# Alternating the two experts' gate and up products, and a new place for the transposed dense input

## The chip, the cores and the metric

The kernel runs on one core of one Trainium2 chip. The metric is the device time of one execution in microseconds. Three timed runs of the kernel before gave 1130.45, 1132.79 and 1132.81 us, so a median of 1132.79 us. The profiled execution took 1131.38 us, and its span from the first to the last instruction is 1129.59 us.

## The reference

A batch of one sequence of 256 tokens of width 1024 passes through two blocks. The first has a gated delta rule and a differential attention side by side, and a dense SwiGLU feed-forward of width 2816. The second has gated linear attention and block attention side by side, then cross attention to a memory, then a mixture of 32 experts, and a last RMS norm. The experts are what the change is about:

```
expert = grp * EXPERTS_PER_GROUP + top_i            # 2 experts per token
hid = jax.nn.silu(xb @ w_gate[e]) * (xb @ w_up[e])  # 1024 -> 512, twice
out += (hid @ w_down[e]) * w[:, None]               # 512 -> 1024
```

Everything is float32. One expert has 3 x 1024 x 512 weights, so the 32 of them are 201 MB, and all of them are read from HBM.

## The kernel before, in words

All tokens sit in two tiles of 128. Up to about 640 us of the span the kernel does the dense work; every weight of it is streamed through three raw buffers (`wr0` to `wr2`, pool `raw`), split into a high and a low part (`wh`, `wl`, pool `hl`, four of each) and multiplied against the transposed input (`xTh`, `xTl`, pool `xt`, eight tiles of 2 KB per partition). These pools, with `cst2`, `m1` and `g1` below them, lie on the left side of SBUF, one above the other in the order in which they are opened.

The experts then run in 16 pairs. Per expert 64 tokens are gathered (`CAP`), so one expert fills half of the 128 output partitions: expert j of a pair writes partitions `H[j]`, 0 to 63 or 64 to 127. For one pair, the loop at line 2197 does:

- at every other pair a `gather` for the next two pairs (`ohr` against `xh` and `xl`), then `hid_T`, the transposes of the hidden rows;
- `gate_up` of the next pair (line 2097): for 8 slices k of 128 input rows, gate (c = 0) and up (c = 1) of both experts, 32 matmuls with 64 columns of `xe` as the weights of the array and 512 columns of expert weights moving. The profile records each of these float32 matmuls as two, so 64 records. After the first quarter of them `between` puts in the `combine` of the pair before (`ys` against `pwT`) and `slots_T`;
- `down` of this pair (line 2121): 16 matmuls (32 records), in the order k, c, j, so that it alternates between the experts.

The last pair has no next one. In its place come `final_gain`, `between` and two fillers (`keep`). After the loop come `combine`, the norm and the stores.

The expert weights arrive in units of 1 MB: four of gate and up (q = 0 to 3, two k each, two transfers of 512 KB) and two of down per expert. They are loaded by SP's queue in the order in which the pairs use them: gate and up of pair p + 1, then down of pair p; within them q by q, first expert 0, then expert 1. The last two units are cut in two halves each. There are 22 slots of 8 KB per partition (tiles `wm`). Four are opened early, five after the mixer, and 13 when the left pools are closed; these 13 (`rawl`, `wm0` to `wm12`) lie over what was `m1`, `g1`, `xt`, `hl` and `raw`. The list at line 804 is the order in which those 13 are filled, and each waits for whoever last used the bytes below it. A unit can only be loaded into a slot when the unit 22 places earlier in the order has been used up.

The order of matmuls on TensorE is that of the program text (no planner acts in the expert part). Every engine instruction is recorded at line 249, since one helper issues them all.

Of the kernel before, what the change touches and what calls it, by code (L numbers as in the profile page):

```python
# [138 lines left out]
RAW = 3  # L139
HLB = 4  # L140
NXT = 8
# [280 lines left out]
class K:  # L422
# [338 lines left out]
    def build(self):  # L761
        tc = self.tc
        with ExitStack() as top:
            P = lambda name, bufs, **kw: top.enter_context(tc.tile_pool(name=name, bufs=bufs, **kw))
            self.c = P("cst", 1)
            psum = P("psum", 1, space=PSUM)
            self.dram = P("dram", 1, space=DRAM)
            self.sm = P("sm", 2)
            work = P("work", 1)
            self.xe = work.tile([128, 8, 4, CAP], F32, name="xe")  # L770
            self.hdT = work.tile([128, 4, 2 * CAP], F32, name="hdT")
            self.sg = work.tile([128, 512], F32, name="sg")
            top.enter_context(tc.manual_schedule())
            self.banks = [psum.tile([128, 512], F32, name=f"bank{i}") for i in range(8)]
            self.freeb, self.turn = list(self.banks), 0
            prj = ExitStack()
            Q = lambda name, bufs: prj.enter_context(tc.tile_pool(name=name, bufs=bufs, side="left"))
            self.c2 = Q("cst2", 1)
            self.M1 = Q("m1", NM1)
            self.G1 = Q("g1", NG1)  # L780
            self.XT = Q("xt", NXT)
            self.hl = Q("hl", 1)
            self.raw = Q("raw", 1)
            with tc.tile_pool(name="g2a", bufs=NG2A, side="right") as self.G2:
                self.rt = None
                self.begin()
                self.block1_attn()
            self.experts = Experts(self, P("early", 1, side="right", reuse_waits="tile"))
            with tc.tile_pool(name="g2", bufs=NG2, side="right", reuse_waits="tile") as self.G2:
                self.S.after = lambda: self.experts.load(min(self.experts.n + NAFT, NRE))  # L790
                self.block1_ffn()
                out = self.mixer()
            self.rt = P("rt", 1, side="right", reuse_waits="tile")
            self.experts.more(P("rawt", 1, side="right", reuse_waits="tile"), reversed(range(NRT)))
            self.S.after = lambda: self.experts.load(self.experts.n + NAFT)
            self.S.after()
            self.drive(self.norm_, [out])
            self.mem_attn()
            prj.close()
            A = P("moe", 1, side="left", reuse_waits="tile")  # L800
            raw = lambda i: 10 + (len(self.S.units) - i) % RAW
            hl = lambda i: 6 + (len(self.S.pieces) - i) % HLB
            self.experts.more(P("rawl", 1, side="left", reuse_waits="tile"),
                              [0, raw(3), raw(2), 5, 4, raw(1), hl(4), hl(3), hl(2), hl(1), 1, 2, 3])
            self.experts.early = False
            self.moe(A)

# [1237 lines left out]
    def moe(self, A):  # L2045
# [51 lines left out]
        def gate_up(n, j0, ws_, between=None):  # L2097

            g = [self.bank() for _ in range(2)]
            for k, j, c in [(2 * q + i, j, c) for q in range(4) for j in range(n) for i in range(2) for c in range(2)]:  # L2100
                if between and (k, j, c) == (2, 0, 0):
                    between()
                self.mm(g[c][H[j]], xe[:, k, j0 + j], ws_(j, k // 2)[:, c, k % 2], k == 0, k == 7)
            sg = self.sg
            R = slice(0, n * CAP)
            nc.scalar.activation(sg[R], g[0][R], AF.Silu)
            V.tensor_tensor(sg[R], g[1][R], sg[R], op=ALU.mult)
            return sg
# [76 lines left out]
        quad = lambda p: rk[:, :, 2 * p:min(2 * p + 4, NE)]  # L2185
        gather(2, self.oh, [x])
        hd = gate_up(2, 0, unit(0))
        for t in range(2):
            nc.scalar.activation(xh[t], x[t], AF.Copy, scale=self.r[:, t:t + 1])
# [7 lines left out]
        for p in range(NP):  # L2197
            n = min(4, NE - 2 * (p + 1))
            if p % 2 == 0 and n:
                gather(n, oh, [xh, xl])  # L2200
            hdT = hid_T(2, hd)
            pw = one_hot(2, col(rk, p), col(W32, p))
            if p % 2 and p + 2 < NP:
                oh = hot(quad(p + 2), min(4, NE - 2 * (p + 2)))

            def between():
                nonlocal pT
                if p:
                    combine(pT)
                pT = slots_T(2, pw)  # L2210
            if n:
                hd = gate_up(2, 2 * (p % 2), unit(p + 1), between)
                X.load(12 * p + 16 + NR)
            else:
                final_gain()
                between()
                keep(NLAST)
            down(2, hdT, unit(p))
            X.load(12 * p + 20 + NR)
# [5 lines left out]
        with tc.If(most > CAP):  # L2225
            with tc.For_i(0, NE, 1) as e:
                one = bass.ds(e, 1)
                rke = A.tile([128, 2, 2], F32, name="rke")
                V.tensor_copy(rke[:, 0, :, None], rk[:, :, one])
                V.tensor_copy(rke[:, 1, :, None], W32[:, :, one])  # L2230
                wu = [X.fetch(spare[q], one, q) for q in range(6)]
                rk_, w_ = (lambda t, j: rke[:, 0, t:t + 1]), (lambda t, j: rke[:, 1, t:t + 1])
                for _ in range(1, T // CAP):
                    V.tensor_scalar(rke[:, 0], rke[:, 0], -float(CAP), None, op0=ALU.add)
                    gather(1, hot(rke[:, 0, :, None], 1), [xh, xl])
                    pT = slots_T(1, one_hot(1, rk_, w_))
                    down(1, hid_T(1, gate_up(1, 0, lambda j, q: wu[q])), lambda j, q: wu[q])
                    for c in range(2):
                        for t in range(2):
                            b = self.bank()  # L2240
                            for i in range(2):
                                self.mm(b, pT[H[0], t * 128:(t + 1) * 128], ys[c][i][H[0]], i == 0, i == 1)
                            sum_ = spare[7 + c][:, t * 512:(t + 1) * 512]
                            nc.scalar.activation(sum_, acc[t][c], AF.Copy)
                            V.tensor_tensor(acc[t][c], b, sum_, op=ALU.add)
            norm_first()
            norm_out()
# [27 lines left out]
```

## Time and profile before

| what | value |
|---|---|
| median of three runs | 1132.79 us |
| profiled execution | 1131.38 us |
| its span | 1129.59 us |
| PE busy | 1107.8 us (98%) |
| DVE, ACT busy | 504.1 us (45%), 381.2 us (34%) |
| read from HBM | 297.83 MB, 265 GB/s over the span |
| gate and up records (`wm`, `xe`) | 1024, first at 640.6 us, last at 1097.2 us |
| down records (`wm`, `hdT`) | 512, first at 682.3 us, last at 1116.4 us |

Busy PE time is a weak measure here: the end of a matmul is modelled, and a matmul on one half of the array counts as busy as two on both halves. What a stretch costs is better read from the starts of what stands before and after it.

### The profile page before, as it was taken

What the parts mean: (1) busy time and instruction counts of PE and PEld (TensorE: products, weight loads), DVE (VectorE), ACT (ScalarE), POOL (GpSimd) and SP (SyncE); (2) the same over time, 40 slices, a digit from 0 to 9 for tenths busy, and PEclk for the clock granted to TensorE, in tenths of its full rate; (3) what the DMA queues carried; (4) which work ended last, traced back from release to release, by engine and by line L of the source; (5) the groups of instructions that cost most, each with busy time, mean ns of one, the idle gap of its engine ahead of it and who ended that gap; (6) DMA issues with size and microseconds to landing.
All of it is one profiled execution on the core that took longest, in us unless ns stands there. A gap on an engine that the chain in (4) does not pass through costs nothing.

```text
span 1129.6 us, 16831 instructions
## 1 busy us (share of the span) xinstructions
PE 1107.8 (98%) x6850; PEld 784.5 (69%) x6850; DVE 504.1 (45%) x917; ACT 381.2 (34%) x678; POOL 57.3 (5%) x85
## 2 busy tenths in 40 slices
PE   9999999999999999999999989999999999999996
PEld 8989788999999887989988644444444445444453
DVE  5777756656556576665666321212121212111112
ACT  6553556544344475565454210000000000000103
POOL 0153011000000010100000000000000000000000
PEclk9999999999999999999999999999999999999999
DMA  8454216674664544545498689999999999999931
GB/s 299 136 165 133 76 38 199 254 246 167 197 189 162 172 150 152 179 126 180 161 359 335 243 337 407 411 413 411 413 412 413 413 413 414 413 413 413 415 156 40
DMA packets 105950, 300.06 MB, mean 266 GB/s; under 512 B 6999, under 2 KB 35980, under 8 KB 97932
## 3 DMA queue, kind: packets, MB, share of 16 engines
q1 hardware_dynamic: 104700, 295.23, 69.6%
q0 software_dynamic: 1024, 3.17, 1.0%
q8 instruction: 56, 0.92, 0.3%
q10 hardware_dynamic: 144, 0.52, 0.1%
q14 instruction: 26, 0.21, 0.1%
HBM read 297.83 MB, written 1.07 MB: 265 GB/s over the span
## 4 chain that ended last, share of the span: by engine, by line
PE 93%; DVE 3%; ACT 2%; issue 1%; DMA 0%; POOL 0%; SPq 0%; ACTq 0%; DVEq 0%
PE bank L249 93%; ACT junk L249 1%; DVE cy L249 0%; DMA x<-in_x 0%; DVE junk L249 0%; DVE xTl L249 0%; ACT wh L249 0%; DVE x L249 0%; DVE xl L249 0%; ACT xTh L249 0%; DVE wm L249 0%; ACT sg L249 0%; DVE dp L249 0%; POOL nr L249 0%; DVE smz L249 0%
## 5 line engine op out<-in xcount | busy, mean ns | idle before, releaser
L249 PE MATMUL bank<-wm,xe 128*64 128x512 f32 x1024 | 285.1, 598 | 0.0
L249 DVE TENSOR_TENSOR wl<-wr,wh 128x1024 fp32r<-128x1024 f32 (+1 forms) x175 | 211.0, 1222 | 134.2 <-ACT wh L249 130.8
L249 PE MATMUL bank<-xTh,wh 128*128 128x256 f32 x768 | 223.1, 291 | 0.0
L249 ACT ACTIVATE wh<-wr 128x1024 fp32r<-128x1024 f32 (+1 forms) x175 | 180.1, 1050 | 118.2 <-PE bank L249 104.6
L249 PE MATMUL bank<-xTl,wh 128*128 128x256 f32 x768 | 217.3, 283 | 0.8 <-DVE xTl L249 0.8
L249 PE MATMUL bank<-xTh,wl 128*128 128x256 f32 x768 | 217.1, 283 | 0.2 <-DVE wl L249 0.2
L249 PEld LDWEIGHTS bank<-wm,xe 128*64 128x64 f32 x1024 | 101.0, 136 | 160.3 <-issue 157.1
L249 PEld LDWEIGHTS bank<-xTh,wh 128*128 128x128 f32 x768 | 147.0, 191 | 4.6 <-issue 2.4
L249 PEld LDWEIGHTS bank<-xTl,wh 128*128 128x128 f32 x768 | 147.1, 192 | 2.3 <-DVE xTl L249 1.2
L249 PEld LDWEIGHTS bank<-xTh,wl 128*128 128x128 f32 x768 | 147.0, 191 | 0.4 <-DVE wl L249 0.4
L249 PE MATMUL bank<-wm,hdT 128*64 128x512 f32 x512 | 128.7, 595 | 0.0
L249 ACT ACTIVATE sg<-bank 128x512 f32<-128x512 f32 x20 | 11.9, 597 | 295.3 <-PE bank L249 295.2
L249 DVE TENSOR_TENSOR sg<-bank,sg 128x512 f32<-128x512 f32 x16 | 11.1, 691 | 191.7 <-PE bank L249 191.7
L249 PEld LDWEIGHTS bank<-wm,hdT 128*64 128x64 f32 x512 | 46.5, 137 | 65.9 <-issue 60.7
L249 DVE SCALAR_TENSOR_TENSOR ys<-bank,ws,ys 128x512 fp32r<-128x512 f32 x32 | 24.0, 751 | 98.8 <-ACT ys L249 96.9
L249 ACT ACTIVATE ys<-bank,ws 128x512 fp32r<-128x512 f32 x32 | 22.0, 688 | 106.1 <-PE bank L249 106.1
L249 DVE TENSOR_SCALAR pwT<-bank 128x256 fp32r<-128x256 f32 x16 | 6.8, 424 | 90.1 <-PE bank L249 90.1
L249 POOL TENSOR_TENSOR nr<-nr,mhalf 128x2 f32<-128x2 f32 (+1 forms) x9 | 6.0, 673 | 713.0 <-DVE nr L249 712.9
L249 PE MATMUL bank<-wl,fhh 128*128 128x512 f32 x88 | 35.2, 400 | 0.0
L249 PE MATMUL bank<-wh,fhh 128*128 128x512 f32 x88 | 34.8, 395 | 0.0
L249 PEld LDWEIGHTS bank<-ys,pwT 128*128 128x128 f32 x128 | 22.8, 188 | 17.2 <-issue 11.4
L249 PE MATMUL bank<-ys,pwT 128*128 128x512 f32 x128 | 34.3, 408 | 0.3 <-DVE ys L249 0.3
(386 smaller groups left out, 1477.0 us busy)
## 6 DMA issues: line engine op xcount, KB each, us to landing
wm<-in_w_exp_gate SPq DMA_DIRECT2D x128, 512.0 KB, 10.2
wm<-in_w_exp_up SPq DMA_DIRECT2D x128, 512.0 KB, 10.2
wm<-in_w_exp_down SPq DMA_DIRECT2D x62, 1024.0 KB, 12.6
wr<-in_w_in SPq DMA_DIRECT2D x33, 1024.0 KB, 5.2
wr<-in_w_gate_up SPq DMA_DIRECT2D x22, 1024.0 KB, 5.7
wr<-in_w_down SPq DMA_DIRECT2D x11, 1024.0 KB, 5.1
wr<-in_w_out SPq DMA_DIRECT2D x8, 1024.0 KB, 5.1
wr<-in_w_ckv SPq DMA_DIRECT2D x4, 1024.0 KB, 6.3
```

What stands on the lines that cost most here:

```text
L249: r = f(*args, **kw)
```

## The change

Two edits. In `gate_up` the 32 matmuls of a pair come in another order: before, for each unit quarter q, all four matmuls of expert 0 and then all four of expert 1; after, for each k and c, one of expert 0 and one of expert 1. The sums that are formed are the same, and `between` stands at the same place (k = 2). The pool `xt` is opened after `hl` and `raw` and not ahead of them, so that it lies above them; the list of the left slots is renumbered so that its entries name the same buffers in the same order.

```
@@ -778,9 +778,9 @@
             self.M1 = Q("m1", NM1)
             self.G1 = Q("g1", NG1)
-            self.XT = Q("xt", NXT)
             self.hl = Q("hl", 1)
             self.raw = Q("raw", 1)
+            self.XT = Q("xt", NXT)
@@ -798,10 +798,10 @@
-            raw = lambda i: 10 + (len(self.S.units) - i) % RAW
-            hl = lambda i: 6 + (len(self.S.pieces) - i) % HLB
+            raw = lambda i: 8 + (len(self.S.units) - i) % RAW
+            hl = lambda i: 4 + (len(self.S.pieces) - i) % HLB
             self.experts.more(P("rawl", 1, side="left", reuse_waits="tile"),
-                              [0, raw(3), raw(2), 5, 4, raw(1), hl(4), hl(3), hl(2), hl(1), 1, 2, 3])
+                              [0, raw(3), raw(2), 12, 11, raw(1), hl(4), hl(3), hl(2), hl(1), 1, 2, 3])
@@ -2097,8 +2097,8 @@
-            for k, j, c in [(2 * q + i, j, c) for q in range(4) for j in range(n) for i in range(2) for c in range(2)]:
-                if between and (k, j, c) == (2, 0, 0):
+            for k, c, j in [(k, c, j) for k in range(8) for c in range(2) for j in range(n)]:
+                if between and (k, c, j) == (2, 0, 0):
                     between()
                 self.mm(g[c][H[j]], xe[:, k, j0 + j], ws_(j, k // 2)[:, c, k % 2], k == 0, k == 7)
```

On TensorE, at the start of `gate_up` of pair 1 (the first of its kind with a `between`), the program's order differs as follows; `wm_5657` is the unit of expert 2, `wm_6218` that of expert 3, `bank_77` takes the gate and `bank_81` the up product.

```order
 L249 MATMUL bank_76<-cst_109,sg 128x128 x4
 L249 MATMUL bank_77<-wm_5657,xe 64x512
+L249 MATMUL bank_77<-wm_6218,xe 64x512
 L249 MATMUL bank_81<-wm_5657,xe 64x512
+L249 MATMUL bank_81<-wm_6218,xe 64x512
 L249 MATMUL bank_77<-wm_5657,xe 64x512
+L249 MATMUL bank_77<-wm_6218,xe 64x512
 L249 MATMUL bank_81<-wm_5657,xe 64x512
-L249 MATMUL bank_77<-wm_6218,xe 64x512
-L249 MATMUL bank_81<-wm_6218,xe 64x512
-L249 MATMUL bank_77<-wm_6218,xe 64x512
 L249 MATMUL bank_81<-wm_6218,xe 64x512
```

The second expert's matmuls have moved up between the first expert's; nothing was added or taken away, and the same happens in all 16 `gate_up`.

On SP's queue, in the first loads into the 13 left slots, before (`wm10` and `wm11` lie over `raw`, `wm5` and `wm4` over `xt`):

```order
L249 DMA wm0_6218<-in_w_exp_up_2 128x1024
L249 DMA wm10_6228<-in_w_exp_gate_2 128x1024
L249 DMA wm11_6229<-in_w_exp_gate_2 128x1024
L249 DMA wm5_6223<-in_w_exp_gate_2 128x1024
L249 DMA wm4_6222<-in_w_exp_gate_2 128x1024
L249 DMA wm12_6230<-in_w_exp_gate_2 128x1024
```

and after (`wm8` to `wm10` over `raw`, `wm12` and `wm11` over `xt`):

```order
L249 DMA wm0_6218<-in_w_exp_up_2 128x1024
L249 DMA wm8_6226<-in_w_exp_gate_2 128x1024
L249 DMA wm9_6227<-in_w_exp_gate_2 128x1024
L249 DMA wm12_6230<-in_w_exp_gate_2 128x1024
L249 DMA wm11_6229<-in_w_exp_gate_2 128x1024
L249 DMA wm10_6228<-in_w_exp_gate_2 128x1024
```

The units come in the same order and over the same buffers; only the addresses differ. (Each row of gate stands ahead of one of up, left out here.)

## Rows read from the trace of the kernel before

**Rows 1.** The page, the span in 40 slices: busy tenths, DMA, GB/s.
```profile
PE   9999999999999999999999989999999999999996
...
DMA  8454216674664544545498689999999999999931
GB/s 299 136 165 133 76 38 199 254 246 167 197 189 162 172 150 152 179 126 180 161 359 335 243 337 407 411 413 411 413 412 413 413 413 414 413 413 413 415 156 40
```
**Rows 2.** Stages: us, busy and count of each engine, granted clock, DMA share, GB/s.
```profile
656.60:660.40 3.80, 0.89 (x4) 0.51 (x3) 3.67 (x4) 1.86 (x2) 0.00 (x0) 0.94 1.02 406
660.40:664.00 3.60, 3.54 (x19) 3.54 (x19) 1.10 (x3) 0.00 (x0) 0.00 (x0) 0.59 1.04 429
680.00:1084.00 404.00, 404.00 (x1727) 182.58 (x1724) 74.31 (x157) 35.45 (x56) 0.00 (x0) 1.00 1.02 412
1085.00:1117.00 32.00, 32.00 (x147) 14.08 (x145) 4.59 (x11) 4.38 (x7) 0.00 (x0) 1.00 0.00 1
```
**Rows 3.** The tile wm: who waited for whom, and counts, ns min/median/max, starts.
```profile
L249 PE MATMUL bank<-wm,xe x1024: 592/592/644, 640.6 to 1097.2; 128*64 128x512 f32 x171
...
L249 PE MATMUL bank<-wm,hdT x512: 592/592/644, 682.3 to 1116.4; 128*64 128x512 f32 x171
...
  DMA wm<-in_w_exp_up: 1.6, 6
```
**Rows 4.** PE in order of time, pairs 14 and 15: start, us, operation, count.
```profile
1077.61 5.42 PE L249 MATMUL bank<-wm,xe 128*64 128x512 f32 x16
1082.96 2.13 PE L249 MATMUL bank<-ys,pwT 128*128 128x512 f32 x8
...
1085.23 11.23 PE L249 MATMUL bank<-wm,xe 128*64 128x512 f32 x45
1095.87 0.64 PE L249 MATMUL bank<-wm,hdT 128*64 128x512 f32 x1
1096.29 0.59 PE L249 MATMUL bank<-wm,xe 128*64 128x512 f32 x1
...
1097.57 7.04 PE L249 MATMUL bank<-wm,hdT 128*64 128x512 f32 x30
1104.54 0.74 PE L249 MATMUL bank<-cst,sg 128*128 128x128 f32 x4
...
1109.94 7.09 PE L249 MATMUL bank<-wm,hdT 128*64 128x512 f32 x32
1117.03 0.50 PE L249 MATMUL bank<-ys,pwT 128*128 128x512 f32 x1
```
**Rows 5.** PE in order of time, pairs 0 to 2.
```profile
640.56 16.06 PE L249 MATMUL bank<-wm,xe 128*64 128x512 f32 x64
...
665.91 5.42 PE L249 MATMUL bank<-wm,xe 128*64 128x512 f32 x16
...
691.61 5.42 PE L249 MATMUL bank<-wm,xe 128*64 128x512 f32 x16
```
**Rows 6.** SP's queue in order of time: start, us, transfers issued.
```profile
631.69 0.97 SPq L249 DMA_DIRECT2D wm<-in_w_exp_up  x1
643.38 0.33 SPq L249 DMA_DIRECT2D wm<-in_w_exp_gate  x1
```
**Rows 7.** SP's queue from 660 us on.
```profile
669.59 2.10 SPq L249 DMA_DIRECT2D wm<-in_w_exp_down  x2
```
**Rows 8.** DMA from 640 to 680 us in 40 slices.
```profile
GB/s 16 0 0 0 135 385 320 229 303 389 406 414 430 410 422 418 401 406 418 414 422 422 434 418 434 328 25 25 0 0 49 246 459 418 401 426 393 340 311 332
```
**Rows 9.** The tile wm from 1060 to 1086 us: last issues, time to landing.
```profile
L249 SPq DMA_DIRECT2D wm<-in_w_exp_down x7: 328/328/328, 1060.7 to 1070.8; - x7
...
DMA to landing us min/median/max: 14.9/16.8/17.4
```
**Rows 10.** The chain that ended last: start, us, what.
```profile
656.73 0.10 DVE sg L249
...
660.46 455.76 PE bank L249 x1940
```

## The prediction

> **What bounds the kernel now.** I read the page's slices first. TensorE looks full over the whole span, and from the 25th slice on the DMA engines are full too, at 411 to 415 GB/s, up to two slices before the end [rows 1]. So in the expert part two resources look like the limit at once, and the question is which one sets the end.
>
> The table by stages answers it. From 680 to 1084 us the transfers run at 412 GB/s with a DMA share of 1.02, without a gap; from 1085 to 1117 us DMA moves nothing and TensorE still has 32 us of work [rows 2]. The last weights are issued at 1070.8 us and land 14.9 us later, at T = 1085.7 us [rows 9]. In the whole stage TensorE waits only a microsecond or two for weights [rows 3], and the chain of waits is one piece of 455.8 us on TensorE from 660.46 us on [rows 10]. So TensorE sets the end, and the transfers finish 31.3 us before its last down product ends at 1117.0 us [rows 4]. From there to the end of the span come 12.6 us (1129.6 - 1117.0) of scaling, combine, norm and stores.
>
> How close the transfers are: 1 MB at 412 GB/s is 2.545 us, so a pair's 12 units need 30.5 us. TensorE takes 29.7 us per pair (first run of `gate_up` from 691.61 to 1077.61 us, 13 pairs) [rows 4, 5]. TensorE lags only because it began with 22 slots full behind it. Any gain on it holds until it has caught up with the transfers.
>
> **The first edit: the order of gate and up.** Each expert uses one half of the array's columns. That the halves run on their own is seen where `gate_up` meets `down`: a down record starts at 1095.87, before a gate and up record at 1096.29 that the program has ahead of it [rows 4]. `down` already alternates, and its 32 records take 7.09 us (1109.94 to 1117.03), 0.222 us each [rows 4]. The first run of `gate_up`, 16 records in blocks of eight per expert, takes 5.35 us (1077.61 to 1082.96), 0.334 us each: expert 1 begins only when much of expert 0's block is done, and runs on alone at the end [rows 4]. The second run, 48 records, takes 12.3 us (1085.23 to 1097.57), so with a fixed part a and b for each 16 records, a + b = 5.35 and a + 3b = 12.34: b = 3.5 us, which is the pace of `down` already, and a = 1.85 us, which is paid once per run. It is this start that alternation can take away. The same operation, shape and type stands in both [rows 3], so I give the alternated `gate_up` the pace of `down`.
>
> - First run: 16 x 0.222 = 3.55 us, for 5.35: 1.80 us less.
> - Second run with the `down` behind it: 48 + 32 records from 1085.23 to 1104.54, 19.31 us [rows 4]; 80 x 0.222 = 17.7 us: 1.6 us less.
> - That is 3.4 us per pair, 15 times. The first `gate_up`, of 64 records, keeps TensorE busy for 16.06 us from 640.56 us on [rows 5]; 64 x 0.222 = 14.2: 1.9 us less.
>
> Together 15 x 3.4 + 1.9 = 53 us of TensorE. If nothing else were late, the last down product would end at 1117.0 - 53 = 1064 us. That is before T, so it can't: the weights are late next. TensorE gains 3.4 us a pair and has 25 us to gain before it waits, so from about the eighth pair on it waits for units.
>
> **When the last weights land then.** The transfers stand still twice before they run full. At 631.69 us SP has filled all 22 slots; the next issue is at 643.38, when the first `gate_up` gives its first slot back [rows 6]. That moment hardly moves: expert 0's first unit is used up after eight records on one half either way. The slots are then given back at about the same pace as before or faster, and 8 MB at 412 GB/s take 20 us, so the transfers run on until 665 to 666 us. There they stop again, for about 5 us (25, 25, 0, 0, 49 GB/s) [rows 8], until the second `gate_up` (from 665.91 [rows 5]) returns a slot: issue at 669.59 us [rows 7]. Between the two lies a chain from the end of the first `gate_up` over `sg`, the copies and the gather [rows 10], which is not changed, so this issue moves with the first `gate_up`: 1.9 to 2.1 us earlier, I take 2.0. Behind it the transfers are full to the end in either kernel, since TensorE gives slots back sooner than before. So T' = 1085.7 - 2.0 = 1083.7 us.
>
> **What is left to do after T'.** The last units are down of pair 14 (four) and of pair 15 (four). The last of pair 14 lands 4 x 2.545 = 10.2 us before T'. The half of `down` that waits for it takes half of 7.0 us: T' - 6.7. Then the unchanged piece from 1104.54 to 1109.94, 5.4 us: T' - 1.3 [rows 4]. `down` of pair 15, 7.0 us: T' + 5.7; its last quarter, which needs the very last transfers, starts at T' + 3.9, so it does not wait. With 12.6 us behind it the span ends at T' + 18.3 = 1102.0 us. `gate_up` of pair 15 is not on this path: its last unit lands 20.4 us before T', and what it then still has to do is a quarter of 14.2 us.
>
> To 1102.0 come the 1.8 us that lie around the span (1131.4 - 1129.6): 1103.8 us by the profiled execution, which itself is 1.4 us below the median. I say 1104.5 us.
>
> **The second edit: addresses.** The order of slots and buffers is the same, so at most a wait changes where a slot straddles two buffers. All of this lies before 631.69 us, and then SP stands for 11.7 us with every slot full [rows 6]. That idle time hides it. Without this cover each microsecond of delay beyond 643.4 us would put T' off by one. I cost it at nothing, with bounds of -0.5 (an earlier fill gives nothing, since slots are full) and +2 us.
>
> **The clock.** After 656.6 us TensorE was busy 0.89 of 3.80 us, and in the next 3.6 us its granted clock was 0.59, so that for part of it it ran at 1.2 and not 2.4 GHz [rows 2]. The changed kernel will wait: for two units, 5.1 us of transfer, it has 3.5 us of work, so 1.6 us idle of 5.1. The Trainium skill, "TensorE: Matmul & The Clock Gate", section "HAM oscillation — how this bites in real kernels", tells of a loop whose products wait for DMA at each step and run slowed down each time. By that the waiting stage would lose its speed where by the rows, with idle pieces of 1.6 us where 2.9 us of idle went ahead of the drop, it keeps it; this is the rival below.
>
> **Rivals.**
> - *The clock falls in the waiting stage, near the end only.* Where TensorE falls behind it has no waits, so the loss heals itself except in the last pieces: 3.5 + 5.4 + 7.0 = 15.9 us after the last down of pair 14 has landed. One short drop as in [rows 2] costs about 2 us; half speed through all of it 15.9: 1106 to 1120 us. For it: the drop seen. Against: shorter waits.
> - *Slower than before: the clock stays down over the whole of pair 15.* From the start of its `gate_up`, some 33 us before T', there are 14.2 (`gate_up`) + 2.3 (`combine` and `slots_T`, 1082.96 to 1085.23) + 7.0 + 5.4 + 7.0 = 36 us of TensorE work [rows 4]; at half speed 72 us, so the last down would end at T' + 39, 33 us later than forecast: 1137 us. It decides once more than 28 us are lost, so nearly all of this stretch must run at 1.2 GHz, though TensorE has no pause in it. That speaks against.
> - *The alternation doesn't do what it is to do.* Inside a run the blocks already go at the pace of `down` (b above); if the start of a run stays, because expert 1's first record waits for something else than its place in the order (its own unit, say), nothing is gained: 1132.8 us. For it: the blocks overlap today. Against: `down`, in the alternated order, shows no such start, 7.09 us for 32 records where a start would make it 8.9.
> - *The transfers bind already*, and the end does not move, 1132.8 us. They are full for 404 us. But they end 31 us before TensorE's last down [rows 2, 4, 9], so T would have to move later by as much.
>
> **How the numbers follow.** Forecast (TensorE catches up, the end is T' + 18.3): 0.86, its own range 1100 to 1107 us, from the bounds -1.5 (the drop of the clock at 660 us, 0.41 of 3.6 us [rows 2], misses the gather) and +2 of the addresses, and 0.5 for the pace of the pieces. Clock near the end: 0.06. No gain from the order: 0.03. Transfers bind already: 0.02. Slower: 0.03. What a measurement of this kernel can tell from no change is about 0.2%. So faster 0.92, same 0.05, slower 0.03. The range for 8 in 10 goes from 1099 to 1112 us, with the smaller clock losses.
>
> **What would show it.** In the profile after: gate and up records of the two experts start in pairs, and the first run takes 3.5 us; from the middle of the stage on TensorE waits for `wm` transfers, 3 to 6 us per pair; the second stop of the transfers ends near 667.6 us; the last weights land near 1083.7 us, and the last down ends about 6 us later, not 31. The granted clock stays at 1.00 from 680 us to the last down. It is wrong if the last landing moves by more than 4 us, if the clock falls in the last 30 us, or if the first run stays above 5 us.

## The result and the profile after

The changed kernel takes 1104.95 us (median of four runs, 1104.13 to 1106.97) against 1132.80 us before (four runs, 1130.45 to 1133.51). The ratio is 0.9756, with a 95% interval from 0.9744 to 0.9768: 28 us faster, 0.5 us from the forecast of 1104.5. The profiled execution took 1105.01 us, with a span of 1103.2 us.

In the page's slices TensorE looks almost as full as in [rows 1]. What they do show is the end: DMA now runs full up to the last slice but one, at 416 GB/s in it.

```profile
PE   9999999999999999999999989999999998989896
...
DMA  8454215676546445463569788999999999999993
GB/s 306 123 185 132 66 54 172 213 274 201 191 154 227 156 127 179 135 206 118 191 219 374 282 321 354 413 414 413 414 412 412 412 411 413 413 412 414 413 416 137
...
PE 73%; DMA 21%; DVE 3%; ACT 2%; issue 1%; POOL 0%; SPq 0%; ACTq 0%; DVEq 0%
```

The last line gives the shares of the chain that ended last. A fifth of it is now transfers; before, the whole expert part was one piece on TensorE [rows 10].

The stages come next; columns as in [rows 2].

```profile
656.60:660.40 3.80, 2.75 (x11) 2.45 (x12) 2.27 (x3) 0.00 (x0) 0.00 (x0) 0.52 1.03 411
660.40:664.00 3.60, 3.60 (x20) 3.60 (x20) 1.57 (x3) 0.00 (x0) 0.00 (x0) 0.56 1.04 426
680.00:880.00 200.00, 200.00 (x982) 85.32 (x980) 43.16 (x92) 19.52 (x31) 0.00 (x0) 1.00 1.02 413
880.00:1084.00 204.00, 186.25 (x852) 75.70 (x850) 35.14 (x76) 18.90 (x30) 0.00 (x0) 1.00 1.01 410
1085.00:1091.00 6.00, 5.82 (x27) 1.77 (x23) 0.69 (x1) 1.25 (x2) 0.00 (x0) 1.00 0.01 3
```

Up to 880 us TensorE is still full. From there to 1084 us it is idle for 17.75 of 204 us, and the transfers stay at 410 GB/s. What remains behind the last transfer is 6 us of TensorE and not 32. Around 660 us the granted clock was at its lower level (half, 1.2 GHz) for twice as long as before; it was 1.00 in the other stages shown.

The tile `wm` tells who waits; the first two rows answer to [rows 3]. The last two are its answer for 1060 to 1086 us alone and answer to [rows 9].

```profile
L249 PE MATMUL bank<-wm,xe x1024: 592/593/644, 640.6 to 1067.7; 128*64 128x512 f32 x171
...
L249 PE MATMUL bank<-wm,hdT x512: 592/593/644, 679.2 to 1089.7; 128*64 128x512 f32 x171
...
  DMA wm<-in_w_exp_down: 38.9, 33
  DMA wm<-in_w_exp_gate: 14.4, 19
  DMA wm<-in_w_exp_up: 8.8, 19
...
L249 SPq DMA_DIRECT2D wm<-in_w_exp_down x6: 327/328/328, 1060.4 to 1069.3; - x6
...
DMA to landing us min/median/max: 14.9/16.8/17.4
```

Waits for weights went from about 2 to 62 us (matmuls and weight loads of the array together, which overlap, so this is more than the idle time). A record lasts as long as before (median 593 ns for 592). The last weights land 1069.3 + 14.9 = 1084.2 us, 1.5 us earlier than before. The last down record starts 27 us earlier (1089.7 for 1116.4).

TensorE in order of time shows the alternation itself, at its first and last use; it answers to [rows 5] and [rows 4].

```profile
640.62 13.95 PE L249 MATMUL bank<-wm,xe 128*64 128x512 f32 x64
656.15 0.36 PE L249 MATMUL bank<-ohr,xh 128*128 128x256 f32 x1 [1.58 <-DVE ohr L249]
657.26 0.58 PE L249 MATMUL bank<-ohr,xl 128*128 128x256 f32 x1 [0.74 <-DVE xl L249]
...
664.86 3.65 PE L249 MATMUL bank<-wm,xe 128*64 128x512 f32 x16
...
686.80 3.65 PE L249 MATMUL bank<-wm,xe 128*64 128x512 f32 x16
...
1057.73 10.52 PE L249 MATMUL bank<-wm,xe 128*64 128x512 f32 x48
1068.08 1.02 PE L249 MATMUL bank<-wm,hdT 128*64 128x512 f32 x2
1069.28 3.65 PE L249 MATMUL bank<-wm,hdT 128*64 128x512 f32 x16 [0.18 <-DMA wm<-in_w_exp_down]
1074.27 3.65 PE L249 MATMUL bank<-wm,hdT 128*64 128x512 f32 x14 [1.33 <-DMA wm<-in_w_exp_down]
1077.84 0.74 PE L249 MATMUL bank<-cst,sg 128*128 128x128 f32 x4
...
1083.24 7.09 PE L249 MATMUL bank<-wm,hdT 128*64 128x512 f32 x32
```

The first run of 16 records takes 3.65 us where it took 5.42. The first `gate_up` takes 13.95 for 16.06 us. From the first run of pair 1 to that of pair 2 it is 686.80 - 664.86 = 21.94 us, before 691.61 - 665.91 = 25.70 [rows 5]: 3.76 us less. At the end, `down` of pair 14 stops twice for its own weights.

The pace of the waiting stage is read from starts of the first run, two pairs apart:

```profile
991.01 3.65 PE L249 MATMUL bank<-wm,xe 128*64 128x512 f32 x16
...
1051.87 3.65 PE L249 MATMUL bank<-wm,xe 128*64 128x512 f32 x16
```

That is 30.4 us per pair, the 30.5 us that a pair's 12 units take by the prediction. From 714.54 to 869.32 us, ahead of the waits, six pairs take 25.8 us each.

### The profile page after: what moved, and what is told of

Read it like the earlier page. It is cut to its first block, busy times and chain, and to the rows that moved or that the text cites. A ratio compares the mean times of both kernels' runs of the same rounds, so it can differ in the third digit from the quotient of the medians.

```text
span 1103.2 us, 16790 instructions
## 1 busy us (share of the span) xinstructions
PE 1063.7 (96%) x6850; PEld 749.7 (68%) x6850; DVE 504.2 (46%) x917; ACT 381.1 (35%) x678; POOL 57.3 (5%) x85
## 4 chain that ended last, share of the span: by engine, by line
PE 73%; DMA 21%; DVE 3%; ACT 2%; issue 1%; POOL 0%; SPq 0%; ACTq 0%; DVEq 0%
PE bank L249 73%; DMA wm<-in_w_exp_up 15%; DMA wm<-in_w_exp_down 5%; ACT junk L249 1%; DVE cy L249 0%; DMA x<-in_x 0%; DVE junk L249 0%; DVE xTl L249 0%; ACT wh L249 0%; DVE x L249 0%; DVE xl L249 0%; ACT xTh L249 0%; DVE wm L249 0%; ACT sg L249 0%; DVE dp L249 0%
## 5 line engine op out<-in xcount | busy, mean ns | idle before, releaser
L249 PE MATMUL bank<-wm,xe 128*64 128x512 f32 x1024 | 230.7, 597 | 4.8 <-DMA wm<-in_w_exp_gate 4.2
L249 PEld LDWEIGHTS bank<-wm,xe 128*64 128x64 f32 x1024 | 71.1, 137 | 141.5 <-issue 120.9
L249 PE MATMUL bank<-wm,hdT 128*64 128x512 f32 x512 | 121.5, 595 | 13.0 <-DMA wm<-in_w_exp_down 12.9
L249 PEld LDWEIGHTS bank<-wm,hdT 128*64 128x64 f32 x512 | 38.0, 137 | 93.3 <-issue 66.8
L249 PE MATMUL bank<-ohr,xh 128*128 128x256 f32 (+1 forms) x128 | 34.2, 303 | 1.6 <-DVE ohr L249 1.6
L249 PE MATMUL bank<-ohr,xl 128*128 128x256 f32 (+1 forms) x128 | 33.8, 300 | 1.1 <-DVE xl L249 1.1
```

The costliest lines, as they stand in the source:

```text
L249: r = f(*args, **kw)
```

## The experiments

Eight kernels were run. The first four shared a chip and runs of the kernel before (median 1133.16 us), the last four another (1132.52 us).

**The order alone (e1_order_only)** and **the addresses alone (e2_pools_only)**. The first is the kernel before with the new loop of `gate_up`; the second is the changed kernel with the old loop.

```
-            for k, j, c in [(2 * q + i, j, c) for q in range(4) for j in range(n) for i in range(2) for c in range(2)]:
+            for k, c, j in [(k, c, j) for k in range(8) for c in range(2) for j in range(n)]:
```

> The kernel before with the new order of gate and up alone; the pools stay where they were. Theory (the order of the products is the whole change): 1105 us, within 1.5 us of the changed kernel, first run of 16 records 3.6 us. Rival (the new addresses carry a part): between 1107 and 1133 us.

> The kernel before with the pool xt moved above hl and raw alone; the old order of gate and up. Theory: 1132.8 us within 1.5 us, since SP has every slot full at 631.7 us and then stands until 643.4 us either way. Rival (the addresses carry a part): below 1131 us, or above 1134.5.

Measured: the order alone 1103.99 us (1102.77 to 1105.09), ratio 0.9744 [0.9728, 0.9760]; the addresses alone 1133.28 us, ratio 0.9996 [0.9987, 1.0006]. The order is the whole gain, and the addresses do nothing that shows (within about 1 us). With them alone SP stands as before: its last issue with every slot full, and the first after it, are these rows of its queue, for [rows 6].

```profile
631.63 0.83 SPq L249 DMA_DIRECT2D wm<-in_w_exp_up  x1
643.25 0.33 SPq L249 DMA_DIRECT2D wm<-in_w_exp_gate  x1
```

The stand of 11.6 us is the cover that the prediction named. It was not needed: the last slot was filled at 631.63 us, for 631.69 before, so the new addresses had not delayed the fill.

**Less work for TensorE, in both kernels (e3_before_less, e4_after_less).** In the `combine` of 13 pairs the products with the low part of `ys` are left out, so this is a test of time alone: it leaves out part of the result.

```
-        def combine(pT, last=False, cs=(0, 1)):
+        def combine(pT, last=False, cs=(0, 1), part=False):
...
-                    for i in range(2):
+                    for i in range(1 if not last and part else 2):
...
-                    combine(pT)
+                    combine(pT, part=p < 14)
```

> The kernel before, in which 13 of the combines leave out the low part of the expert outputs (4 of their 8 products of 0.216 us, so 0.87 us of TensorE per pair, 11.2 us in all). Theory (TensorE sets the end before the change): 1121 to 1123 us. Rival (the transfers bind already): 1132.8 us.

> The changed kernel with the same products left out of 13 combines, 11.2 us less of TensorE work. Theory (TensorE has caught up, the end is the last landing plus about 18.5 us): 1105 us within 1.5 us, waits for weights 10 us longer in sum. Rival (TensorE still sets the end): 1094 us.

Measured: before with the cut 1119.72 us, ratio 0.9877 [0.9861, 0.9894], 13.4 us less and below the 1121 to 1123 us expected. In its trace a pair takes 0.92 us less, 13 times 12.0 us, and the last `down` ends at 1105.03 us, 12.0 us earlier than before (1117.03). The other 1.4 us stand between medians alone; the 13 runs of the kernel before on this chip spread over 2.6 us. After with the cut 1104.38 us, ratio 0.9750 [0.9734, 0.9767], not to be told from after (0.9756). So TensorE's work sets the end before the change and no longer does after it. Where the saved time went is seen in what the array's weight loads wait for. First after, then after with the cut (us in total, times, longest):

```profile
PEld bank L249 <- DMA wm<-in_w_exp_down: 26.0, 21, 2.2
PEld bank L249 <- DMA wm<-in_w_exp_gate: 10.2, 16, 3.0
PEld bank L249 <- DMA wm<-in_w_exp_up: 8.2, 16, 1.1
```

```profile
PEld bank L249 <- DMA wm<-in_w_exp_down: 33.2, 19, 3.5
PEld bank L249 <- DMA wm<-in_w_exp_gate: 11.3, 12, 1.9
PEld bank L249 <- DMA wm<-in_w_exp_up: 9.4, 14, 1.1
```

The work that was left out came back as waits for weights: these rose from 44.4 to 53.9 us, and those of the matmuls themselves from 17.6 to 24.6. The two kinds overlap, so their sum is more than the 12 us left out. The pace shows it without that doubt: with the cut, too, a pair of the waiting stage takes 30.4 us, for 30.4 in after.

```profile
990.36 3.65 PE L249 MATMUL bank<-wm,xe 128*64 128x512 f32 x16
...
1051.12 3.65 PE L249 MATMUL bank<-wm,xe 128*64 128x512 f32 x16
```

**Blocks of two (e5_blocks_two).** The changed kernel with two matmuls of one expert (gate and up of one k), then two of the other. It asks why a run had a start of 1.85 us at all: does each block cost something, or does only the part of a block that TensorE can't look past?

```
-            for k, c, j in [(k, c, j) for k in range(8) for c in range(2) for j in range(n)]:
+            for k, j, c in [(k, j, c) for k in range(8) for j in range(n) for c in range(2)]:
```

> The changed kernel with the order k, expert, c: two products (four records) of one expert, then two of the other, so blocks half as long as before the change. Theory A (TensorE looks ahead of a half that is busy by some four records, so that a block of eight holds the other half up and a block of four does not): first run of 16 records 3.5 to 3.8 us, 1105 us. Theory B (the second half always starts a block late): the start costs half of the 1.85 us of before, first run 4.4 to 4.6 us; the time then still near 1104 to 1106 us, since the weights come no earlier.

Measured in one run: 1105.51 us (before: 1132.52). The first runs of pairs 1 and 2, in order of time:

```profile
665.76 3.70 PE L249 MATMUL bank<-wm,xe 128*64 128x512 f32 x16
669.39 0.44 PE L249 MATMUL bank<-cst,oh 128*128 128x128 f32 x2
...
687.84 3.81 PE L249 MATMUL bank<-wm,xe 128*64 128x512 f32 x16
```

Blocks of four records keep nearly the full pace, 3.70 and 3.81 us against 3.65; blocks of eight took 5.42. So it is not the block as such that costs, and a look-ahead of limited reach fits the start. The single records of the kernel before show it directly: in the run from 1077.61 us expert 0's records start every 0.429 us, and expert 1's first one starts at 1079.379, 6 ns behind expert 0's fifth, so with three of expert 0's still to start. With blocks of two matmuls it starts 0.164 us behind expert 0's first (688.001 for 687.837), again with three of that block to start, and in the changed kernel 7 ns behind it (1051.879 for 1051.872). What sets this reach was not tested.

**The work behind the last units (e6_gain_early).** In the changed kernel `final_gain` and the work that depends on it on other engines (2 us on TensorE) are issued ahead of `down` of pair 14, where TensorE waits for weights, and no longer behind it.

```
             else:
-                final_gain()
                 between()
                 keep(NLAST)
+            if p == NP - 2:
+                final_gain()
             down(2, hdT, unit(p))
```

> The changed kernel with final_gain (2.0 us of TensorE between the last two down products) moved ahead of down of pair 14, into the time in which TensorE waits for the last weights. Theory (the end is the last landing plus the TensorE work that is left after the last down of pair 14 has landed): 2.0 us less, 1102 to 1103.5 us. Rival (the tail is not bound by that work): 1105 us.

Measured: 1102.56 us (1100.00 to 1102.85), ratio 0.9727 [0.9706, 0.9749].

```profile
1068.71 2.05 PE L249 MATMUL bank<-g,cst 8*128 8x128 f32 x16
1070.68 7.65 PE L249 MATMUL bank<-wm,hdT 128*64 128x512 f32 x32
...
1081.58 7.09 PE L249 MATMUL bank<-wm,hdT 128*64 128x512 f32 x32
```

The 2 us now lie in what was waiting time. `down` of pair 14 runs in one piece, only 0.6 us longer than without waits (7.65 for 7.04), since nearly all of its weights have landed by then, and `down` of pair 15 starts 3.1 us ahead of the last landing (1084.66), where it was 1.0 us in after. Counted from the landing, that is a gain of 2.1 us. The landing itself came 0.5 us later in this run, and the last `down` starts 1.7 us earlier than in after. The intervals of the two ratios overlap a little, so by the times alone the gain is likely rather than certain.

**The second stop of the transfers (e7_split_early).** In the changed kernel the split of the tokens into `xh` and `xl` and the one-hot of the next pairs (`ohr`), on which the gather waits, are issued ahead of the first `gate_up`.

```
         gather(2, self.oh, [x])
-        hd = gate_up(2, 0, unit(0))
         for t in range(2):
...
+        hd = gate_up(2, 0, unit(0))
```

> The changed kernel with the split of the dense input (xh, xl) and the one-hot of the next pairs computed ahead of the first gate_up and not behind it, so that TensorE goes from the first gate_up to the gather without the idle piece of about 4 us. Theory (the second stop of the transfers ends when the second gate_up gives back its first slot, and that waits for this idle piece and for the half clock behind it): the stop of some 3.5 us near 667 us goes, last landing 3 to 5 us earlier, 1100 to 1102 us. Rival (the transfers do not gain from it): 1105 us.

Measured: 1101.40 us (1101.21 to 1102.49), ratio 0.9724 [0.9706, 0.9742]. DMA from 640 to 680 us in 40 slices, first in after (for [rows 8]), then in this kernel:

```profile
GB/s 102 4 0 0 94 356 348 238 291 344 401 418 418 426 406 418 422 401 406 414 426 434 410 426 434 401 66 8 0 106 254 410 434 418 430 385 401 410 434 414
```

```profile
GB/s 0 0 0 0 74 319 410 287 213 360 389 397 422 422 418 426 406 406 410 418 414 422 442 410 418 401 426 434 426 418 401 401 414 406 410 414 410 401 414 418
```

The stop near 667 us is gone, and the last weights land at 1080.5 us, 3.7 us earlier than in after. TensorE goes from the first `gate_up` into the gather without a pause and stays at the full clock, and the second `gate_up` starts at 659.17 us (664.86 in after):

```profile
654.63 0.40 PE L249 MATMUL bank<-ohr,xh 128*128 128x256 f32 x1
...
659.17 3.65 PE L249 MATMUL bank<-wm,xe 128*64 128x512 f32 x16
...
1076.77 3.20 PE L249 MATMUL bank<-ys,pwT 128*128 128x512 f32 x8
...
1081.08 7.09 PE L249 MATMUL bank<-wm,hdT 128*64 128x512 f32 x32
```

The third row (2.13 us elsewhere) shows a stretch at half clock, 3.4 us long, in the piece between the two last `down`; the last `down` therefore starts 0.6 us behind the landing. That this profiled run took 1102.49 us and the other three 1101.21 to 1101.41 may be this, which one trace can't prove.

**Both moves (e8_both).** The edits of e6_gain_early and e7_split_early together.

> Both of the moves (final_gain into the wait, split ahead of the first gate_up). Theory: they add, 5 to 7 us less than the changed kernel, 1098 to 1100.5 us. Rival: only one of them shows, 1100 to 1103 us.

Measured: 1099.07 us (1098.47 to 1100.15), ratio 0.9707 [0.9688, 0.9726]: the fastest of all, ahead of the kernel before by 33 us and of the changed one by about 6. `down` of pair 15 begins at 1076.98 us, 3.0 us ahead of the last landing at 1080.0 (last issue 1065.1, 14.9 us), as in e6_gain_early, and the stop of the transfers is gone as in e7_split_early. TensorE in order of time at the end:

```profile
1064.12 2.05 PE L249 MATMUL bank<-g,cst 8*128 8x128 f32 x16
1066.10 7.64 PE L249 MATMUL bank<-wm,hdT 128*64 128x512 f32 x32
...
1076.98 7.09 PE L249 MATMUL bank<-wm,hdT 128*64 128x512 f32 x32
```

Between the two `down` lies the same piece as in e6_gain_early, all of it 4.6 us earlier. By the medians against the changed kernel's 1104.95 us (from another chip) the gains are 2.4 us (e6_gain_early), 3.6 (e7_split_early) and 5.9 (both), so they add up within the noise of about 1 us; the one moves what lies behind the last landing and the other the landing itself.

## Why the prediction was right

*The bound before.* TensorE, with 31 us of it behind the last weights: confirmed by e3_before_less, where 12.0 us of work taken from TensorE alone, with no transfer changed, moved the end of the last `down` by 12.0 us.

*The gain per pair.* Sized at 3.4 us; between pairs 1 and 2, where nothing waits yet, it is 3.76 us. The first run, from its first record to the work behind it, fell by 1.77 us (5.35 to 3.58; 1.80 forecast), the first `gate_up` by 2.1 (1.9 forecast); the second run with `down` fell by 1.99 (19.31 to 17.32; 1.6 forecast). The alternated records go at 0.215 us each (starts 0.429 us apart on either half); the 0.222 read from `down` had the hand-over to the next work in it. The rival that a run's start stays fell with that.

*The catch-up.* TensorE waits for weights from about 889 us on, in `down` of pair 8, which is the ninth pair; about the eighth had been forecast. The forecast divided 25 us by 3.4 us a pair and left out that TensorE, at 29.7 us a pair for the transfers' 30.5, was already gaining 0.8 us a pair on them. An estimate with that, from the prediction's own figures: (25 + 15 x 0.8) / (3.4 + 0.8) is 8.8 pairs. Of waits 3 to 6 us per pair had been forecast: 30.4 for 25.8 us a pair is 4.6 us. In the windows of one pair's length (30.5 us) from 884 and from 1014 us TensorE is idle for only 2.8 and 3.9 us, since one half runs on while the other waits, as at 889 us for two records.

*The last landing.* Forecast 1083.7 us, a shift of 2.0; the shift was 1.5. The second stop ends with the issue at 668.54 us, where 667.6 was forecast; SP's queue in order of time, for [rows 7]:

```profile
668.54 0.81 SPq L249 DMA_DIRECT2D wm<-in_w_exp_down  x2
```

The term that was mis-sized is "this issue moves with the first `gate_up`: 1.9 to 2.1 us earlier". The first `gate_up` did end 2.1 us earlier; but the half clock behind it lasted 6.8 us, not 3.4, and held nearly the whole gather. The second `gate_up` started only 1.05 us earlier (664.86 for 665.91). The other runs point the same way, by the length of the half clock at this place and the last landing:

| order | half clock near 660 us | last landing, us |
|---|---|---|
| old | 3.4 us | 1085.7 (before), 1086.5 (e2_pools_only), 1087.1 (e3_before_less) |
| new | 6.8 us | 1084.2 (after), 1085.2 (e5_blocks_two), 1084.7 (e6_gain_early) |
| new | 3.4 us | 1083.5 (e4_after_less) |
| new | none | 1081.9 (e1_order_only) |

At an equal 3.4 us the new order moves the landing by 2.2 to 3.6 us, more than the 2.0 forecast; at 6.8 us part of it is lost again. The landings of one row differ by up to 1.4 us, and the rows with 3.4 us and with none hold one run each, so the trend is likely and its size is not settled. In e1_order_only the second `gate_up` started at 662.52 us. The prediction's bound for the clock, -1.5 us, was one-sided: it allowed the half clock to go, and not to double.

*What is left behind the last landing.* Forecast 18.3 us, measured 1103.2 - 1084.2 = 19.0. The forecast let `down` of pair 14 wait only in its second half; the trace has it stop after 2 and again after 18 of its 32 records, and `down` of pair 15 begin 1.0 us ahead of the landing, where T' - 1.3 was the forecast. That the piece between the two (5.4 us) lies on the path is what e6_gain_early shows: there 2.1 us of it were moved off.

*The end as a minimum.* What TensorE saved, forecast at 53 us and by the starts nearer 58 (15 x 3.75 + 2.1), became 28 us, and the rest became waits. That is the prediction's main step, and e4_after_less shows it: 12 us less work in the same kernel change nothing clear of the noise.

*The second edit.* Nothing within about 1 us, by e2_pools_only, and the fill was not delayed at all.

*The clock.* By the granted clock the waiting stage kept 1.00 in after. The Trainium skill's rule for loops that wait for DMA at each step ("TensorE: Matmul & The Clock Gate", "HAM oscillation — how this bites in real kernels") does not describe this stage: the products wait in every pair, the longest idle stretch of TensorE in after was 2.15 us (ending at 910.71), and the clock fell only around 660 us. Four of the other kernels had one more stretch of 3.4 us at half clock. Two of them lie in the waiting stage, each behind the longest wait of its kernel: at 909 us in e1_order_only (2.40 us idle) and at 922 us in e4_after_less (2.65 us idle); waits followed that could take them up. In e6_gain_early 2.57 us of idle (ending at 911.47) were followed by no fall. The other two, at 1077 us in e7_split_early and, with the old order and no pause ahead of it, at 1107 us in e2_pools_only, came right behind the small products of `final_gain`, and each made the piece ahead of the last `down` 1.6 us longer (6.96 for 5.40 us). So the rival of small losses near the end was a true possibility, and cheap. The slower case did not come up in any run.

The match of the total is partly luck. The landing moved by 1.5 us for 2.0, and 19.0 us lie behind it for 18.3; these two errors add up to 1.2 us, the difference between 1105.0 us in the profiled execution and the 1103.8 of the sum. The 0.7 us that the forecast put on top, because the profiled execution before lay below its median, hid part of that: after the change the profiled execution does not lie below the median (1105.01 for 1104.95). The low end of the forecast's own range, 1100 us, does not come out of the bounds named for it: 1104.5 less 1.5 and 0.5 is about 1102.5 us.

## What to carry to other kernels

When TensorE is full and the transfers are full too, compare the moment at which the last weights land with the last product: the distance is all that a faster TensorE can give, and behind it the gain turns into waits. After that, look for what still moves the last landing (a stop of the transfers early in the stage) and for work that can go from behind the last transfer into the waits ahead of it; here these two gave another 6 us together. Matmuls that fill half the columns should, as far as this kernel shows (float32, 512 columns moving), alternate between the halves every one or two instructions, not every four.

## What the runs showed of the hardware

- In blocks of eight the second half of the columns was not begun until the first half had started its fifth record: these blocks (four float32 matmuls) paid 1.85 us per run, blocks of four (two matmuls) 0.05 to 0.16 us, alternation nothing. Within this reach records of the two halves start out of program order, as [rows 4] show at 1095.87 us.
- The half clock after the pauses around 656 us was not the same from kernel to kernel with nearly the same pauses. Pauses of 1.54 to 1.58, 0.74 and about 0.7 us (the last 0.40 in the changed kernel, whose clock was down already) were followed by 6.8 us of it in the changed kernel and e6_gain_early, 3.4 in the one before, e2_pools_only, e3_before_less and e4_after_less, and none in e1_order_only. In e5_blocks_two the first pause was 2.09 us, and 6.8 us followed. What decides between these was not found. With no pause there was none (e7_split_early, e8_both).
- One core's transfers held 410 to 413 GB/s for 400 us in a row, whether TensorE waited or not.
